# Two-layer encoder: six pairs of each MLP begin with two of their seven products, and the loads, splits and stores around the MLPs are re-timed

## The chip, the cores and the metric

One core of a Trainium2 chip runs the whole program: TensorE (PE, with PEld its weight loads), VectorE (DVE), ScalarE (ACT), GpSimd (POOL), and the queue of SyncE (SP), which issues nearly all DMAs. The metric is the device time of one execution in microseconds (us), lower is better. Durations of single instructions, waits and clocks come from one profiled execution.

## The reference

```python
def reference(x, c, positions, ada_w, ada_b, norm_mix, norm_mlp, mlp_w1, mlp_w2, ...):
    cond = jax.nn.silu(c)
    for i in range(DEPTH):                       # 2 layers, SEQ = 1024, D_MODEL = 1024, D_FF = 4096
        mod = (cond @ ada_w[i] + ada_b[i]).reshape(B, N_MOD, D)
        shift1, scale1, gate1 = ...
        shift2, scale2, gate2 = ...
        h = rms_norm(x, norm_mix[i]) * (1 + scale1) + shift1
        if i % N_MIXERS == 0:
            y = mla_mixer(h, positions, ...)     # layer 0, ends with "@ w_o"
        else:
            y = dilated_mixer(h, positions, ...) # layer 1: three window groups, bias by relative position
        x = x + gate1 * y
        h = rms_norm(x, norm_mlp[i]) * (1 + scale2) + shift2
        x = x + gate2 * (jnp.square(jax.nn.relu(h @ mlp_w1[i])) @ mlp_w2[i])
    return x
```

All tensors are float32.

## The kernel before

**Products.** Each float32 factor is split into a rounded part `hi` (ACT, L114) and a rest `lo` (DVE, L115), and a product is three TensorE passes (lines L383, L384, L385: hi by hi, lo by hi, hi by lo). Such a split is called a form here. A product of 128 columns by 512 tokens over 512 inner elements is 12 matmuls of 128x512.

**The MLP** (`mlp7`) does each 2x2 block product with seven products instead of eight. `prod` names them: L11·R11, L12·R21, S4·R22, L22·T4, S1·T1, S2·T2, S3·T3. In the first phase ("up") the left side is w1 and the right side the normalised input h. A pair is 256 columns of w1 (128 of them in each half); there are 16 pairs, and each takes the seven products in the order L11·R11, S2·T2, L12·R21, S3·T3, S1·T1, L22·T4, S4·R22 (index 0 to 6). S1 to S4 are sums of quarters of w1 (`w_sums`, four DVE operations of 128x512 per pair), T1 to T4 are differences of quarters of h. The sums u of squared results that the second phase needs (`u_sums`, four DVE operations per pair) go to a DRAM scratch `uf` (`u_store`, four DMAs per pair). In the second phase ("down") 56 steps (7 products by 8 groups of w2) each load a part of `uf` ("ufr") and of w2 ("w2r"), split them (`d_form`) and run 24 matmuls.

**The way into the MLP.** `proj_res` is the mixer's last projection. When a tile of 128 tokens is finished it adds the gate and the residual, normalises, and hands out steps made by `h_forms` that transpose and modulate the tile: `first` for the first four tiles, `second` for tiles 4 to 7. `second` computes also all of T1 to T4's differences, and `form`s make the splits of R11, R21, T2, R22, T1, T3, T4. Before, w1 of pairs 0 and 1 is loaded ahead but split behind the projection; pairs 0 and 1 then alternate their products, and from pair 2 on the pairs run one after the other.

**What sets the order.** Code order within each engine's stream, as a scheduler keeps it where an operation is pinned and else by its own choice. Tiles come from a "G" pool of 29 tiles and an "X" pool of 19 (layer 0) or 20 (layer 1), each 128x1024 float32; a new user of a tile waits for the last reader of the old one, and SP issues its DMAs in order, so a store that is not ready holds back the loads behind it.

**Work spread over the MLP of layer 0:** `ada_step` (one 512 KB load "adaw" and one or two DVE operations of 128x1024, the modulation of layer 1), `bias_step` and `write` (DMAs between `bias`, `f` and `bv`, the position bias of layer 1). In the down phase these are a list by step, `fill`. The first three sets of weights of the dilated mixer (`wvr`, `wqkr`) are loaded and split by `dil`, behind the MLP.

Of the kernel before, what the change touches and what calls it, by code (L numbers as in the profile page):

```python
# [41 lines left out]
class K:  # L42
# [284 lines left out]
    def h_forms(self, xs0, xs1, mods, xalloc):  # L327
# [8 lines left out]
        tt = lambda o, x, y: nc.vector.tensor_tensor(o, x, y, op=ALU.subtract)  # L336

        def form(name, src):
            g = [self.G("hf", (P, 2, 512)) for _ in range(2)]
            self.split(*g, src)  # L340
            for k in range(2):
                R.setdefault(name, [[], []])[k].append(g[k])
# [520 lines left out]
    def proj_res(self, O, order, wo, gate, xs, mods, xalloc, done):  # L863
# [4 lines left out]
        with self.tc.tile_pool(name="psO", bufs=6, space=PSUM, reuse_waits="tile") as psp:  # L868
# [29 lines left out]
            for i, (t, b) in enumerate(items):  # L898
# [6 lines left out]
                for _ in range((0, 2, 2, 2, 2, 0, 0, 0)[i]):  # L905
                    steps.pop(0)(psp, "h")
        return at, (at1, steps1)


    def mlp7(self, l, R, steps, xd, out, more=(), nxt=None):  # L910
# [15 lines left out]
        with self.tc.tile_pool(name="psM", bufs=8, space=PSUM, reuse_waits="tile") as psp:  # L926
# [20 lines left out]
            def w_form(L, n):  # L947
                g = self.X("wf", (P, 2, 4, P))
                self.split(g[:, 0], g[:, 1], L[n])
                L[n] = g  # L950

# [3 lines left out]
            def up(u, i):  # L955
# [12 lines left out]
                if i == 0:  # L968
                    u.s1 = self.T("s1")
                    nc.scalar.activation(u.s1, ps, AF.Copy)  # L970
                elif i == 1:
                    u.u2 = self.T("u2")
                    tt(u.u2, ps, u.s1)
                elif i == 2:
                    u.a = self.X("ua", (P, 2, 512), F32)
                    square(u.a[:, 0], ps, u.s1)
# [20 lines left out]
            def u_store(u, c):  # L997
                for n, x in ((("L11", "S1"), u.a), (("L12", "L22"), u.b), (("S3", "S2"), u.s)):
                    nc.sync.dma_start(out=uf[UF[n[0]] : UF[n[0]] + 2, c].rearrange("k p f -> p k f"), in_=x)
                nc.sync.dma_start(out=uf[UF["S4"], c], in_=u.s4)  # L1000
# [45 lines left out]
            def u_forms(c, names):  # L1046
                for n in names:
                    w_form(us[c].L, n)


            us = [Pair() for _ in range(NP)]
            names = [o[0] for o in order]
            raws = {c: w_load(c) for c in range(2)}

            def quarters(c):
                us[c].L = w_quarters(raws.pop(c))
                us[c].q = dict(us[c].L)

            def sums(c):
                w_sums(us[c].L, us[c].q)  # L1060

            for c in range(2):
                quarters(c)
            for n in ("L11", "L12"):
                for c in range(2):
                    u_forms(c, (n,))
            for f in ((0, 0), (1, 0), None, (0, 2), None, (1, 2), None, None):
                if f:
                    up(us[f[0]], f[1])
                else:  # L1070
                    steps.pop(0)(psp, "m")
            for c in range(2):
                sums(c)
                u_forms(c, ("S2",))
            todo = (1, 3, 4, 5, 6)
            for j, i in enumerate(todo):
                up(us[0], i)
                if steps:
                    steps.pop(0)(psp, "m")
                if j < 4:  # L1080
                    for c in range(2):
                        u_forms(c, (names[todo[j + 1]],))
# [709 lines left out]
def program(tc, a):  # L1792
    nc = tc.nc
    with ExitStack() as ctx:
# [35 lines left out]
        with tc.tile_pool(name="bias", bufs=1) as bp:  # L1830
# [17 lines left out]
            for f in fill[16:]:  # L1848
                f.append(write)
# [77 lines left out]
```

## Time and profile before

| | |
|---|---|
| median of 3 runs | 3534.16 us (3531.26 to 3534.18) |
| the profiled execution | 3527.56 us |
| its span on the core | 3525.8 us, mean granted TensorE clock 0.977 |
| TensorE busy | 3330.1 us, 94% |
| VectorE, ScalarE, GpSimd busy | 2476.0, 1769.5, 764.5 us |
| up phase of layer 0, layer 1 | about 835 to 1176 us, 2871 to 3211 us |
| down phase of layer 0, layer 1 | about 1177 to 1518 us, 3211 to 3518 us |
| DMA traffic | 482.91 MB, mean 137 GB/s |

The profile gives, for each instruction group, its line in the source, the busy time and the mean duration of one. "Idle before" is the time its engine stood still just before it, with the engine and line that ended the wait. The table by stages gives for each window the busy time of each engine, the granted clock of TensorE (1.00 is full speed) and the share of the 16 DMA engines in use. "SPq" and "POOLq" are the DMA-issuing queues of SyncE and GpSimd.

### The profile page before, as it was taken

To read this page: it belongs to the slowest core of one execution; us is meant where nothing else is said; L and a number is where in the kernel's file an instruction comes from. 1 tells how busy PE (TensorE), PEld (TensorE's weight loads), DVE (VectorE), ACT (ScalarE), POOL (GpSimd) and SP (SyncE) were. 2 spreads that over 40 slices of the span, in tenths; PEclk is the share of its full clock that TensorE was granted. 3 is DMA by queue.
4 is the path that set the end of the run, shared out by engine and by line. 5 is a ranking of instruction groups with operands and counts; after the bars stand their busy time and mean duration, and the time that the engine had idled before them with its cause. 6 is when DMAs were issued, how large, how long until landed. Compare 5 with 4: busy or idle time off the path is not lost.

```text
span 3525.8 us, 58151 instructions
## 1 busy us (share of the span) xinstructions
PE 3330.1 (94%) x21350; PEld 2971.2 (84%) x21350; DVE 2476.0 (70%) x4860; ACT 1769.5 (50%) x3559; POOL 764.5 (22%) x1299
## 2 busy tenths in 40 slices
PE   6999999897999898989999999999999779999999
PEld 6877788776888786889999999999999668887887
DVE  6678787856887766756667666676778577777666
ACT  5557676744554333535556454564555245454332
POOL 6454444420000000012222222233333200000000
PEclk9999999998999999999999999999999889999999
DMA  5442222241545789533332333332334624447464
GB/s 185 131 163 78 75 93 73 91 138 66 188 170 174 265 211 340 169 88 106 104 99 80 98 106 94 112 87 65 102 97 125 169 84 145 151 162 277 169 213 138
DMA packets 376557, 482.91 MB, mean 137 GB/s; under 512 B 31077, under 2 KB 256658, under 8 KB 376266
## 3 DMA queue, kind: packets, MB, share of 16 engines
q1 hardware_dynamic: 366186, 453.88, 40.3%
q0 software_dynamic: 10080, 25.24, 2.1%
q8 instruction: 171, 2.80, 0.3%
q14 instruction: 120, 0.98, 0.1%
HBM read 348.71 MB, written 118.79 MB: 133 GB/s over the span
## 4 chain that ended last, share of the span: by engine, by line
PE 77%; DVE 6%; DMA 4%; ACT 3%; issue 2%; SPq 0%; POOL 0%; DVEq 0%; ACTq 0%; POOLq 0%
PE psm L385 10%; PE psm L384 10%; PE psm L383 10%; PE psproj L383 8%; PE psproj L385 7%; PE psproj L384 7%; PE pav L804 3%; PE pss L1526 2%; PE ppt L791 2%; PE pspt L1552 2%; PE psq L1495 2%; PE psy L385 2%; PE psy L383 2%; PE psy L384 2%; PE psav L1567 1%
## 5 line engine op out<-in xcount | busy, mean ns | idle before, releaser
L383 PE MATMUL psm<-hf,wf 128*128 128x512 f32 x896 | 354.0, 395 | 24.7 <-ACT wf L114 24.6
L384 PE MATMUL psm<-dl,dh 128*128 128x512 f32 x896 | 354.3, 395 | 11.8 <-DVE dl L115 11.8
L385 PE MATMUL psm<-hf,wf 128*128 128x512 f32 x896 | 351.6, 394 | 11.1 <-DVE wf L115 11.1
L383 PE MATMUL psm<-dh,dh 128*128 128x512 f32 x896 | 339.5, 396 | 18.1 <-ACT dh L114 18.1
L385 PE MATMUL psm<-dh,dl 128*128 128x512 f32 x896 | 352.6, 393 | 0.0
L384 PE MATMUL psm<-hf,wf 128*128 128x512 f32 x896 | 352.5, 393 | 0.0
L383 PE MATMUL psproj<-wqkh,hTp 128*128 128x256 f32 x1024 | 296.8, 290 | 0.0
L385 PE MATMUL psproj<-wqkh,hTp 128*128 128x256 f32 x1024 | 291.5, 285 | 0.0
L384 PE MATMUL psproj<-wqkl,hTp 128*128 128x256 f32 x1024 | 289.9, 283 | 0.0
L114 ACT ACTIVATE dh<-ufr 128x1024 fp32r<-128x1024 f32 x112 | 118.6, 1059 | 284.6 <-DMA ufr<-uf 113.7
L383 PEld LDWEIGHTS psm<-hf,wf 128*128 128x128 f32 x896 | 170.7, 190 | 63.1 <-ACT wf L114 28.3
L383 PEld LDWEIGHTS psm<-dh,dh 128*128 128x128 f32 x896 | 170.1, 191 | 57.8 <-ACT dh L114 21.5
L384 PEld LDWEIGHTS psm<-dl,dh 128*128 128x128 f32 x896 | 170.7, 191 | 50.8 <-DVE dl L115 15.3
L385 PEld LDWEIGHTS psm<-hf,wf 128*128 128x128 f32 x896 | 170.3, 190 | 49.2 <-DVE wf L115 13.7
L115 DVE TENSOR_TENSOR dl<-ufr,dh 128x1024 fp32r<-128x1024 f32 x112 | 136.6, 1220 | 100.5 <-ACT dh L114 86.3
L780 POOL TENSOR_SCALAR p<-p,arl 128x1024 f32<-128x1024 f32 x128 | 145.0, 1133 | 268.9 <-DVE arl L779 204.6
L385 PEld LDWEIGHTS psm<-dh,dl 128*128 128x128 f32 x896 | 170.7, 190 | 35.5
L384 PEld LDWEIGHTS psm<-hf,wf 128*128 128x128 f32 x896 | 170.7, 190 | 35.3
L384 PEld LDWEIGHTS psproj<-wqkl,hTp 128*128 128x128 f32 x1024 | 195.8, 191 | 0.0
L385 PEld LDWEIGHTS psproj<-wqkh,hTp 128*128 128x128 f32 x1024 | 195.6, 191 | 0.0
L1537 ACT ACTIVATE pd<-pd,dnb 128x192 f32<-128x192 f32 (+2 forms) x384 | 168.5, 443 | 54.0 <-DVE dnb L1535 54.0
L383 PEld LDWEIGHTS psproj<-wqkh,hTp 128*128 128x128 f32 x1024 | 195.6, 191 | 0.0
(354 smaller groups left out, 9809.0 us busy)
## 6 DMA issues: line engine op xcount, KB each, us to landing
ufr<-uf SPq DMA_DIRECT2D x112, 512.0 KB, 3.9
adaw<-in_ada_w SPq DMA_DIRECT2D x96, 512.0 KB, 7.1
w2r<-in_mlp_w SPq DMA_DIRECT2D x96, 512.0 KB, 5.0
w1r<-in_mlp_w SPq DMA_DIRECT2D x64, 512.0 KB, 5.8
bt<-bias SPq DMA_DIRECT2D x128, 256.0 KB, 2.7
wqkr<-in_dil_w_in SPq DMA_DIRECT2D x96, 256.0 KB, 4.0
qkv<-st SPq DMA_DIRECT2D x32, 512.0 KB, 3.4
hraw<-qkv SPq DMA_DIRECT2D x32, 512.0 KB, 3.9
```

Of the source, the lines that this page charges most:

```text
L114: nc.scalar.activation(hi, src, AF.Copy)
L115: (lo_eng or nc.vector).tensor_tensor(lo, src, hi.bitcast(F32), op=ALU.subtract)
L383: mm(out, lh, rh, start=first, stop=False)
L384: mm(out, lh, rl, start=False, stop=False)
L385: mm(out, ll, rh, start=False, stop=last)
L780: nc.gpsimd.tensor_scalar(p, p, rl, 1.0, op0=ALU.mult, op1=ALU.mult)
L791: nc.tensor.transpose(pt[:, k * P : (k + 1) * P], u["p"][i][:, kt * P : (kt + 1) * P], self.ident)
L804: nc.tensor.matmul(ps[:, j % 2, :], heads[h]["v"][:, kt, :], u["pT"][hl][kt // 4][:, kt % 4, :], start=kt == 0 and hl == 0, stop=kt == 7 a ...
L1495: nc.tensor.transpose(ps[:, (2 * e + k) * P : (2 * e + k + 1) * P], s4[:, i, e, 64 * k : 64 * k + 128], identr)
L1526: nc.tensor.matmul(ps[:, e * 256 : (e + 1) * 256], q[:, e, k, :], u["k"][:, e, w0 : w0 + 256], start=k == 0, stop=k == 1)
L1537: nc.scalar.activation(p[:, e, lo:hi], p[:, e, lo:hi], AF.Exp, bias=nb[:, e : e + 1], accum_out=stat[g][:, t, 1, 2 * pr + e : 2 * pr + e + 1])
L1552: nc.tensor.transpose(ps[:, (n * e + b) * P : (n * e + b + 1) * P], p[:, e, c : c + P], self.ident)
```

## The change

It is made for both MLPs.

- **Six early pairs.** For pairs 0 to 5 the left half of w1 that the quarters L11 and L12 need is loaded once more by itself ("w1h", 128 columns of all 1024 rows, 512 KB), and split into the G pool. The first three are loaded at step 3 of the projection's second loop and split at its steps 4, 5 and 6 (`more`).
- **Order of products.** `seq`: first L11·R11 and L12·R21 of pairs 0 to 5 (12 products), then the other five products of each of these pairs, then pairs 6 to 15 with seven each. All loads, sums and forms are put by product number: w1 of a pair 12 products ahead, its sums 6 ahead, a form 4 ahead.
- **T2 first.** `second` computes only T1's and T2's difference and the form of T2; the differences of T3 and T4 are in `others`, with the forms of T3, T1, T4, R22. The steps stand at products 2, 3 (`second`), 5, 7, 8, 10 (`others`). These operations are pinned.
- **Stores of u** go out from GpSimd's queue.
- **Down phase.** Loads are issued three steps ahead instead of two, the first four near the end of the up phase, the first two forms at its last two products. The loads of x for the residual are spread over four steps, the gate comes at group 4.
- **Layer 0's extra work.** Up phase: one `ada_step` for pairs 3 to 15. Down phase: `ada_step` at steps 8 to 40, none at 0 to 7; bias steps at 8 and 13 instead of 1 and 6; writes at 16 to 23 and 40 to 47 instead of from 16 on.
- **Dilated weights.** `wv` loaded at down step 51 and split at 53, `wqk` loaded at 54.

```diff
         def second(psp, tag, dp):
-            t1, t4 = keep[dp], keep[2 + dp]
-            t3, r22, t2 = (xalloc("hs", (P, 2, 512), F32) for _ in range(3))
-            rs.append((t3, r22))
+            t1 = keep[dp]
+            t3, r22 = (xalloc("hs", (P, 2, 512), F32) for _ in range(2))
+            t2 = self.G("ht2", (P, 2, 512), F32)
+            rs.append((t3, r22, t2))
...
             tt(t1, t3, t1)
             tt(t2, r22, t1)
-            form("T2", t2)
-            tt(t3, r22, t3)
-            tt(t4, t4, t2)
+            form("T2", t2, True)
 
         def others(name):
-            for src in {"T3": [r[0] for r in rs], "T1": keep[0:2], "T4": keep[2:4], "R22": [r[1] for r in rs]}[name]:
-                form(name, src)
+            for dp in range(2):
+                t3, r22, t2 = rs[dp]
+                if name == "T3":
+                    tt(t3, r22, t3)
+                elif name == "T4":
+                    tt(keep[2 + dp], keep[2 + dp], t2)
+                form(name, {"T3": t3, "T1": keep[dp], "T4": keep[2 + dp], "R22": r22}[name], True)
...
+    def w1_half(self, l, c):
+        src = self.a["mlp_w1"][l].rearrange("(d p) f -> p d f", p=P)[:, :, c * 256 : c * 256 + P]
+        return self.load(src, (P, 8, P), "w1h")
+
+    def w1_form(self, src, alloc):
+        g = alloc("wf", (P, 2, 4, P))
+        self.split(g[:, 0], g[:, 1], src)
+        return g
...
             def u_store(u, c):
                 for n, x in ((("L11", "S1"), u.a), (("L12", "L22"), u.b), (("S3", "S2"), u.s)):
-                    nc.sync.dma_start(out=uf[UF[n[0]] : UF[n[0]] + 2, c].rearrange("k p f -> p k f"), in_=x)
-                nc.sync.dma_start(out=uf[UF["S4"], c], in_=u.s4)
+                    nc.gpsimd.dma_start(out=uf[UF[n[0]] : UF[n[0]] + 2, c].rearrange("k p f -> p k f"), in_=x)
+                nc.gpsimd.dma_start(out=uf[UF["S4"], c], in_=u.s4)
...
+            seq = [(c, i) for c in range(E) for i in (0, 2)]
+            seq += [(c, i) for c in range(NP) for i in range(7) if c >= E or i not in (0, 2)]
...
+            for c in range(E):
+                if eloads[c]:
+                    put(2 * c - 5, eloads[c])
+                if eforms[c]:
+                    put(2 * c - 3, eforms[c])
+            for n, f in zip((2, 3, 5, 7, 8, 10), steps):
+                put(n, f, psp, "m")
+            for c in range(NP):
+                put(first[c] - 12, quarters, c)
+                put(first[c] - 6, quarters, c)
+                for i in range(7):
+                    if not (c < E and i in (0, 2)):
+                        put(at[(c, i)] - 4, form, c, i)
+                put(at[(c, 6)] + 2, u_sums, us[c])
+                put(at[(c, 6)] + 4, u_store, us[c], c)
+                if l == 0 and 2 < c < NP:
+                    put(at[(c, 4)], self.ada_step, psp, "m")
+            for k in range(4):
+                put(N - 6 + k, d_first, k, False)
+            for k in range(2):
+                put(N - 2 + k, d_first, k, True)
...
-                if n + 2 <= last:
-                    ld[n + 2] = d_load(*dsteps[n + 2])
-                for k in {last - 2: (last - 1, last), last - 1: (), last: ()}.get(n, (n + 1,)):
+                if n > 0 and n + 3 <= last:
+                    ld[n + 3] = d_load(*dsteps[n + 3])
+                for k in {0: (), last - 2: (last - 1, last), last - 1: (), last: ()}.get(n, (n + 1,)):
...
-            fill = [[k.ada_step] if n < 8 or n >= 16 else [] for n in range(54)]
+            fill = [[k.ada_step] if 8 <= n < 41 else [] for n in range(56)]
...
-            for n in (1, 6):
+            for n in (8, 13):
                 fill[n].append(bias_step)
-            for f in fill[16:]:
+            for f in fill[16:24] + fill[40:48]:
                 f.append(write)
+            fill[51].append(lambda *x: got.update(wv=k.dil_weights("v", 0, 0)))
+            fill[53].append(lambda *x: got.update(wv=got["wv"]()))
+            fill[54].append(lambda *x: got.update(wqk=k.dil_weights("qk", 0, 0)))
...
-            k.mlp7(1, forms, steps, xm[1], store, [[k.ada_step]] * 8 + [[]] * 8 + [[k.ada_step]] * 3)
+            k.mlp7(1, ea, forms, steps, xm[1], store, [[]] * 8 + [[k.ada_step]] * 11)
```

**Where it moves instructions, first place: ACT at the end of layer 0's projection.** Lines L259, L104, L105 normalise one tile of tokens (xh); L114 wf is the rounded part of a quarter of w1, from `w1r` (256 columns) or `w1h` (128 columns). Before:

```order
L259 ACTIVATE xh_15230,xms_15229<-x_14675 128x1024
L104 ACTIVATE xrl_15233<-xms_15229,eps 128x1
L105 ACTIVATE xry_15232<-xrl_15233 128x1
L259 ACTIVATE xh_15273,xms_15272<-x_14677 128x1024
L104 ACTIVATE xrl_15276<-xms_15272,eps 128x1
L105 ACTIVATE xry_15275<-xrl_15276 128x1
L259 ACTIVATE xh_15316,xms_15315<-x_14679 128x1024
L104 ACTIVATE xrl_15319<-xms_15315,eps 128x1
L105 ACTIVATE xry_15318<-xrl_15319 128x1
L114 ACTIVATE wf_15347<-w1r_15339 128x512
L114 ACTIVATE wf_15350<-w1r_15343 128x512
```

Now:

```order
L340 ACTIVATE hf_15203<-hk_15195 128x1024
L114 ACTIVATE wf_15207<-w1h_15141 128x512
L114 ACTIVATE wf_15210<-w1h_15141 128x512
L114 ACTIVATE wf_15256<-w1h_15143 128x512
L114 ACTIVATE wf_15259<-w1h_15143 128x512
L114 ACTIVATE wf_15305<-w1h_15145 128x512
L114 ACTIVATE wf_15308<-w1h_15145 128x512
L259 ACTIVATE xh_15242,xms_15241<-x_14675 128x1024
L104 ACTIVATE xrl_15245<-xms_15241,eps 128x1
L105 ACTIVATE xry_15244<-xrl_15245 128x1
L259 ACTIVATE xh_15291,xms_15290<-x_14677 128x1024
```

Six splits of w1 that stood behind the normalisation of the last tile stand ahead of that of the last three tiles.

**Second place: DVE in the first products of layer 0's MLP.** L336 are the differences of quarters of h, L115 (now also L341) hf the rests of their forms, L919 (now L955) ws the sums of w1's quarters and ua results of products. Before:

```order
L919 TENSOR_TENSOR ua_15489<-psm_15476,s_3169_15387 128x512
L919 TENSOR_TENSOR ws_15509<-w1r_15339,w1r_15341 128x512
L919 TENSOR_TENSOR ws_15510<-w1r_15339 128x512
L336 TENSOR_TENSOR hk_15189<-hk_15189,hs_15443 128x1024
L115 TENSOR_TENSOR hf_15471<-hs_15443,hf_15470 128x1024
L115 TENSOR_TENSOR hf_15494<-hs_15389,hf_15493 128x1024
L919 TENSOR_TENSOR ws_15509<-ws_15509,w1r_15339 128x512
L115 TENSOR_TENSOR hf_15498<-hs_15441,hf_15497 128x1024
L115 TENSOR_TENSOR hf_15502<-hk_15039,hf_15501 128x1024
L115 TENSOR_TENSOR hf_15506<-hk_15084,hf_15505 128x1024
L919 TENSOR_TENSOR ws_15510<-w1r_15341,ws_15509 128x512
```

Now:

```order
L336 TENSOR_TENSOR hk_15084<-hs_15456,hk_15084 128x1024
L955 TENSOR_TENSOR ws_15558<-w1r_15363,w1r_15365 128x512
L955 TENSOR_TENSOR ws_15559<-w1r_15363 128x512
L336 TENSOR_TENSOR ht_3189_15458<-hs_15457,hk_15084 128x1024
L955 TENSOR_TENSOR ws_15558<-ws_15558,w1r_15363 128x512
L955 TENSOR_TENSOR ua_15518<-psm_15542,ua_15518 128x512
L955 TENSOR_TENSOR ws_15559<-w1r_15365,ws_15558 128x512
L341 TENSOR_TENSOR hf_15486<-ht_3189_15458,hf_15485 128x1024
L115 TENSOR_TENSOR wf_15520<-w1h_15454,wf_15520 128x512
L115 TENSOR_TENSOR wf_15523<-w1h_15454,wf_15523 128x512
L336 TENSOR_TENSOR hs_15400<-hs_15401,hs_15400 128x1024
L955 TENSOR_TENSOR ua_15577<-psm_15593,ua_15577 128x512
```

The sums of the first pair stand before the last form of T2 now, and the long operations on h are taken apart by short ones on w1 and on results.

**Third place: SP's queue at the end of layer 0's up phase.** L999 and L1000 are stores of u, L234 an `ada_step`'s load, L389 (now L396) the loads of u and w2. Before:

```order
L999 DMA uf_15335<-ub_17899 128x2x512
L999 DMA uf_15335<-ua_17867 128x2x512
L999 DMA uf_15335<-us_17949 128x2x512
L1000 DMA uf_15335<-us_3616_17950 128x512
L234 DMA adaw_17959<-in_ada_w 128x1024
L389 DMA ufr_17962<-uf_15335 128x2x512
L389 DMA w2r_18055<-in_mlp_w 128x2x512
L389 DMA w2r_18057<-in_mlp_w 128x2x512
L389 DMA w2r_18097<-in_mlp_w 128x2x512
L389 DMA w2r_18099<-in_mlp_w 128x2x512
```

Now:

```order
L234 DMA adaw_17890<-in_ada_w 128x1024
L396 DMA ufr_17893<-uf_15359 128x2x512
L396 DMA w2r_17895<-in_mlp_w 128x2x512
L396 DMA w2r_17897<-in_mlp_w 128x2x512
L396 DMA w2r_18006<-in_mlp_w 128x2x512
L396 DMA w2r_18008<-in_mlp_w 128x2x512
L396 DMA w2r_18045<-in_mlp_w 128x2x512
L396 DMA w2r_18047<-in_mlp_w 128x2x512
L396 DMA w2r_18084<-in_mlp_w 128x2x512
L396 DMA w2r_18086<-in_mlp_w 128x2x512
```

The stores are gone from this queue (GpSimd issues them), and the loads of w2 no longer stand behind the last pair's results.

More of the change, by code (lines that the diff above doesn't have):

```diff
@@ L861, in wo_load, with proj_res @@
         return self.wsplit(src, (P, 2, 512), "wo", alloc=alloc)
-    def proj_res(self, O, order, wo, gate, xs, mods, xalloc, done):
+    def proj_res(self, O, order, wo, gate, xs, mods, xalloc, done, more):
         nc = self.nc
@@ L906, in proj_res, with mlp_early, load, form @@
                     steps.pop(0)(psp, "h")
+                for f in more.get(i, ()):
+                    f()
         return at, (at1, steps1)
-    def mlp7(self, l, R, steps, xd, out, more=(), nxt=None):
+    def w1_half(self, l, c):
[5 more added lines that the diff above has]
+        return g
+    def mlp_early(self, l, E):
+        Ls, raws = [{} for _ in range(E)], {}
+        def load(c):
+            raws[c] = self.w1_half(l, c)
+        def form(c):
+            raw = raws.pop(c)
+            for g in range(2):
+                Ls[c][f"L1{g + 1}"] = self.w1_form(raw[:, 4 * g : 4 * g + 4, :], self.G)
+        return Ls, [lambda c=c: load(c) for c in range(E)], [lambda c=c: form(c) for c in range(E)]
+    def mlp7(self, l, early, R, steps, xd, out, more=(), nxt=None):
         nc, a = self.nc, self.a
@@ L1044, in down @@
                     self.mm3(ps, uh[:, k, ts], ul[:, k, ts], wh[:, k, :], wl[:, k, :], first and k == 0, last and k == 1)
-            def u_forms(c, names):
-                for n in names:
-                    w_form(us[c].L, n)
+            Ls, eloads, eforms = early
+            E = len(Ls)
             us = [Pair() for _ in range(NP)]
[L1052 to L1074, printed above, removed]
@@ L1167, in mlp7 @@
                     ps = [M() for _ in range(4)]
[L1168 to L1172 removed]
+                if i in (3, 5) and gr < 4:
+                    t = i * 2 - 6 + gr
+                    xs[t] = self.load(xd[t * P : (t + 1) * P, :], (P, 1024), "x")
+                if (i, gr) == (3, 4):
+                    g = self.gate(l, 1)
                 if (i, gr) == (5, 5) and nxt is not None:
@@ L1826, in program, with early @@
         keep_x = lambda l: (lambda t: nc.gpsimd.dma_start(out=xm[l][t * P : (t + 1) * P, :], in_=xs[t]))
-        forms, (_, steps) = k.proj_res(O, (4, 5, 0, 1, 2, 3, 6, 7), wo, gate, xs, mods(0, 3), k.X, done=keep_x(0))
+        got = {}
+        def early(l, E=6, n=3):
+            Ls, loads, forms = k.mlp_early(l, E)
+            hooks = {3: loads[:n]}
+            for c in range(n):
+                hooks[4 + c] = [forms[c]]
+            return (Ls, [None] * n + loads[n:], [None] * n + forms[n:]), hooks
+        ea, hooks = early(0)
+        forms, (_, steps) = k.proj_res(O, (4, 5, 0, 1, 2, 3, 6, 7), wo, gate, xs, mods(0, 3), k.X, keep_x(0), hooks)
         xd = k.dp.tile([S, D], F32, name="xd")
@@ L1856, in program @@
         wo = {0: [], 1: []}
-        got = {}
         def tail():
@@ L1873, in program @@
                 nc.sync.dma_start(out=xs[t][p0 : p0 + n, :], in_=s)
-        forms, (_, steps) = k.proj_res(O, range(8), wo, got["gate"], xs, mods(1, 3), k.X, done=keep_x(1))
+        ea, hooks = early(1)
+        forms, (_, steps) = k.proj_res(O, range(8), wo, got["gate"], xs, mods(1, 3), k.X, keep_x(1), hooks)
         def store(t, c, x, eng):
```

168 lines of the change are left out of this document (75 added, 93 removed).

## The prediction
> **What bounds the kernel now.** I read the page's first part, then the table by stages around the MLPs, then TensorE's waits, its timeline and the chain of waits there, and last the DMA rows.
>
> ```profile
> PE 3330.1 (94%) x21350; PEld 2971.2 (84%) x21350; DVE 2476.0 (70%) x4860; ACT 1769.5 (50%) x3559; POOL 764.5 (22%) x1299
> ```
>
> TensorE is busy 94% of the span. The change leaves its number of matmuls as it is, so only time in which it stands still, or runs slowly after standing still, can be won. That time lies in six stretches:
>
> ```profile
> 830.00:880.00 50.00, 31.97 (x128) 24.43 (x127) 37.90 (x48) 26.77 (x40) 0.53 (x1) 0.76 0.14 45
> 1160.00:1215.00 55.00, 45.23 (x178) 35.81 (x177) 43.16 (x55) 18.86 (x22) 0.00 (x0) 0.88 0.77 279
> 1300.00:1360.00 60.00, 48.38 (x192) 36.84 (x191) 25.07 (x25) 12.82 (x13) 0.00 (x0) 0.91 0.98 289
> 1495.00:1535.00 40.00, 28.30 (x135) 23.76 (x134) 26.84 (x36) 17.89 (x27) 1.48 (x3) 0.87 0.40 130
> 2866.00:2912.00 46.00, 28.27 (x114) 21.15 (x113) 36.79 (x47) 26.76 (x40) 0.53 (x1) 0.78 0.23 76
> 3195.00:3230.00 35.00, 27.00 (x102) 21.06 (x102) 26.37 (x27) 14.90 (x17) 0.00 (x0) 0.85 0.94 355
> ```
>
> Length less PE busy is TensorE's idle time: **A** (layer 0, projection to MLP) 18.0 us, **C** (up to down) 9.8, **D** (middle of down) 11.6, **E** (MLP to dilated mixer) 11.7, **B** (layer 1, projection to MLP) 17.7, **F** (up to down) 8.0. Together 76.8 us. The column after POOL is the granted clock: 0.76 to 0.91 here. The timeline and the chain of waits of A show what that costs and why it waits:
>
> ```profile
> 862.42 0.80 PE L383 MATMUL psm<-hf,wf 128*128 128x512 f32 x1 [8.39 <-ACT wf L114]
> 863.01 0.63 PE L384 MATMUL psm<-hf,wf 128*128 128x512 f32 x1
> 868.71 0.80 PE L385 MATMUL psm<-hf,wf 128*128 128x512 f32 x1 [5.07 <-DVE wf L115]
> ```
> ```profile
> 841.97 0.43 PE psm L384
> 842.40 2.06 PE pst L290 x16
> 844.46 0.24 PE psm L383
> 844.71 0.23 PE psm L384
> ...
> 852.20 1.24 DVE hk L336
> ...
> 858.83 2.27 DVE hf L115 x2
> 861.10 0.60 DVE ws L919
> 861.70 3.41 DVE hf L115 x3
> 865.11 1.80 DVE ws L919 x3
> 866.91 1.14 DVE hf L115
> 868.05 0.61 DVE wf L115
> ```
>
> A matmul takes 0.43 us after a wait and 0.23 us otherwise, so a slow one costs 0.20. In A the timeline has 13 slow ones from 836.91 and 11 from 868.71: 24 x 0.20 = 4.9 us. Busy time x (1 - clock) would be 31.97 x 0.24 = 7.7 there, so I take 4.9/7.7 = 0.64 of that figure elsewhere: C 3.5, D 2.8, E 2.4, B 4.0, F 2.6. Slow matmuls cost about 20 us, and **97 us are at stake**.
>
> **The change part by part.** Durations come from the one profiled execution (3527.56 us, span 3525.8). The median of the runs is 3534.16, 6.6 us more; the sum is made against 3527.6.
>
> *A and B.* The wait of 8.39 us is for a quarter sum's split, and 5.07 for its rest. VectorE was never idle: long operations on h (1.14 us each: 3.41 for three) stood in its queue ahead of short ones on w1 (0.60: 1.80 for three). The first products need R11 and R21 alone. Before, four such products (10.9 us with 12 x 0.227 each) covered the making of T2; now twelve do, 12 x 12 x 0.227 = 32.7 us, plus 32 transposes at 2.06 for 16 = 4.1, so from about 832 to 869. VectorE reached T1's difference at 852.2; from there T1 and T2 (four operations) and the two rests of T2's form are 6 x 1.14 = 6.8 us, with some ten short ones 13 us: 865, ahead of 869, and sooner where the first half is transposed sooner. The first wait, 3.8 + 0.7 us for splits that stood behind the last normalisation, goes because three pairs are split within the projection.
>
> What is late next: T3, T1, T4, R22 want 12 x 1.14 = 13.7 us of VectorE while five products last 13.6. Over the whole stretch to pair 5's end TensorE has 42 x 2.72 + 4 = 118 us of work; VectorE has 18 x 1.14 = 20.5, some 128 short operations x 0.60 to 0.64 = 77 to 82, and in layer 0 three `ada_step`s of 1.2: 98 to 106 us, or 83 to 90%. It fits, but not in every product. From nothing to 10 us per layer; I take 3 where T forms follow each other and 2 in the pairs behind. A: 18.0 + 4.9 - 5 = **18**; B: 17.7 + 4.0 - 5 = **17**. The extra loads (12 x 0.5 MB) come where DMA share is 0.14 to 0.23 in A and B's rows, and cost nothing unless they hold a tile; the six splits ahead of the last three normalisations in ACT (0.6 each, 3.6 us) are covered by the same twelve products, and cost up to 3.6 without them.
>
> *C and F.*
>
> ```profile
> SPq L999 <- ACT ub L966: 11.8, 1, 11.8
> ```
> ```profile
> 1174.13 2.58 SPq L389 DMA_DIRECT2D w2r<-in_mlp_w  x4
> ```
> ```profile
> 1180.00:1190.00 10.00, 8.47 (x37) 6.63 (x35) 7.06 (x7) 3.62 (x4) 0.00 (x0) 0.96 1.05 393
> ```
>
> SP's queue stood 11.8 us at a store of u, and so issued four loads of w2 only at 1174.13, when the up phase ended at about 1176; from there the DMAs were full (1.05, 393 GB/s). A down step of the first eight loads 0.5 MB of u, 1 MB of w2 and 0.5 MB of adaw in 5.45 us (24 x 0.227): 367 GB/s, nearly all that row shows. Now the stores are in another queue, the loads can start some 10 to 20 us earlier, as soon as TensorE frees X tiles, and without adaw in steps 0 to 7 the need is 275 GB/s. I leave 2 us in each: C 9.8 + 3.5 - 2 = **11**, F 8.0 + 2.6 - 2 = **9** (ends: 4 and 13).
>
> The store itself has no row on GpSimd. The nearest, issues with KB and us to landing:
>
> ```profile
> xm<-x POOLq DMA_DIRECT2D x16, 512.0 KB, 3.2
> oT<-oTd POOLq DMA_DIRECT2D x12, 512.0 KB, 13.0
> oT<-moTd POOLq DMA_DIRECT2D x8, 512.0 KB, 8.8
> xd<-x POOLq DMA_DIRECT2D x12, 256.0 KB, 3.2
> ```
> ```profile
> uf<-ua SPq DMA_DIRECT2D x32, 512.0 KB, 4.2
> ```
> ```profile
> 1470.00:1500.00 30.00, 30.00 (x150) 25.03 (x148) 30.00 (x41) 18.34 (x26) 2.16 (x4) 1.00 0.62 211
> ```
>
> From 3.2 (the same size and direction) to 13.0 us; SP's own store took 4.2. I take 3.2 to 4.2, and no cost: xd's stores fall in 1470 to 1500, where VectorE is busy 30.00 of 30 us, and still land in 3.2. The Trainium skill ("SBUF — State Buffer", section "SBUF: two separate sides") speaks against this edit: GpSimd writes the descriptors of its own DMAs, and is locked out while VectorE runs an operation in a two-port mode, which a float32 copy within SBUF sets off. By that rule the stores would be late whenever VectorE is so occupied; the rows of xd show no lateness, and the groups of the chain above are TENSOR_TENSOR rather than copies. I give the rule a small chance, below.
>
> *D.*
>
> ```profile
> 1329.90 11.90 DMA f<-bv
> ...
> 1341.86 12.40 DMA w2r<-in_mlp_w
> ```
> ```profile
> 1340.00:1350.00 10.00, 4.76 (x15) 3.83 (x16) 3.94 (x4) 2.11 (x2) 0.00 (x0) 0.66 1.07 330
> ```
>
> ```profile
> w2r<-in_mlp_w SPq DMA_DIRECT2D x96, 512.0 KB, 5.0
> ```
>
> The chain there is DMA after DMA: a bias write, then a w2 load of 12.4 us, against a median of 5.0 for w2r, with the DMA share above 1. Before, one write stood in each of steps 16 to 31, beside x, gate and adaw. Now eight of the 16 go to steps 40 to 47; x is spread, and loads are issued a step (5.45 us) earlier. But eight writes still stand ahead of step 24, and adaw's loads stay. Between 0 and all of it stays; I leave 5: 11.6 + 2.8 - 5 = **9**. Steps 40 to 47 have room (DMA share 0.62 in the row of 1470 to 1500).
>
> *E.*
>
> ```profile
> 1521.18 6.94 DMA wvr<-in_dil_w_in
> 1528.15 1.06 ACT wvh L114
> ```
>
> TensorE waited 11.2 us for these weights, issued at 1521.18 behind the MLP's last rows. Loaded at step 51 they are there some 15 us before. Next late is the transposes of tiles 4 to 7, whose normalisation ends at about 1527; 96 matmuls on the first tiles, which start 0.12 us apart in the timeline, 11.5 us, cover that from 1518. The price: two rests of the split (2 x 1.2 us) enter VectorE while it is busy 30.00 of 30, and delay down's last steps by about as much. I leave 4: 11.7 + 2.4 - 4 = **10** (ends 5 and 14).
>
> *Sum:* 18 + 17 + 11 + 9 + 9 + 10 = **74 us**: 3527.6 - 74 = 3453.6 for a profiled execution. Set against the median it would be 3460; between the two I say **3456 us**.
>
> **The rivals.**
>
> 1. *VectorE becomes the bound behind the projection.* The T forms come one product apart, and the 13.7 us of T3 to R22 show on TensorE as gaps between the products of pair 0, with slow matmuls behind each. For: 37.90 us busy of 50 in A, most of the idle rest at its start. Against: the sum of 83 to 90%. Price: 13.7 more per layer and 5 for the clock, less the 5 left already: 2 x 14 = 28, so 3484.
> 2. *The stores from GpSimd are late, and the kernel is slower.* Four stores end a pair's life in the X pool, in 7 x 2.72 = 19.0 us. If GpSimd handles them one after the other, they keep up as long as one takes under 19.0/4 = 4.75 us. At the 8.8 of oT's row a pair would last 35 us, and 26 pairs would lose 16 each, over 400 us; the loss exceeds the gain of 74 from 5.5 us per store on (4 x 5.5 - 19 = 3, x 26 = 78). Just above that, at 6 us, it is 5 x 26 = 130 less 74: 3590. Against: 3.2 in both rows of stores; oT's are loads, in another stage. This is also the way in which the Trainium skill's rule of the shared port would come out.
> 3. *The DMA stalls only move.* D stays whole (the eight writes ahead of step 24 make a stall of the same size, or those at 40 to 47 do) and C and F keep half: 9 + 10 = 19 lost, 3475.
> 4. *The change doesn't do what it says*: the early halves of w1 wait for G tiles, arrive late, and ACT, which keeps its order, holds the last normalisations behind them. A and B then stay: 35 lost, 3491. Against: before A DMA share is low (0.14 within it), and the tiles are freed by TensorE's first loop in the projection, some 20 us ahead of need.
>
> **How the numbers follow.** The forecast's own range, 3430 to 3472 (nothing left in the pairs and E's and C's upper ends, or 4 us more left in four places), gets 0.60. Rival 1 has 0.14, rival 3 has 0.10, rival 4 has 0.09, rival 2 has 0.04, and 0.03 is for nothing gained on balance. The range 3428 to 3496 reaches from nearly all of the 97 us to rival 4. About 0.2%, or 7 us, is what a measurement of this kernel can tell from no change; faster gets the forecast and rivals 1, 3 and 4, 0.93; same 0.03; slower 0.04.
>
> **What would show it.** A and B right: in the table by stages TensorE is busy at least 45 of 50 us behind each projection, and no wait over 2 us for a w1 split; wrong (rival 1): waits on VectorE's hf or wf rests of 1 to 3 us each between products 13 and 25. C and F right: w2r issued 10 us or more before up ends, no wait over 2 us at the first down steps. The stores: uf rows under POOLq with under 4.75 us to landing; wrong if w1r issues wait for them. D: the wait near step 28 at most 5 us, none at 40 to 47. E: psproj follows the last psm within 1 us. The prediction is wrong as a whole if TensorE's busy time grows (its clock falls elsewhere), or if waits of the same sum stand in other places.

## The result, and the profile after

| | before | changed |
|---|---|---|
| median | 3534.17 us (3531.26 to 3534.22, 4 runs) | 3446.89 us (3443.34 to 3447.82, 4 runs) |
| profiled execution | 3527.56 us | 3447.27 us |
| its span | 3525.8 us | 3444.2 us |

The ratio is 0.9753 with a 95% interval of 0.9736 to 0.9770: 87 us less by the medians, 80.3 by the profiled executions. The forecast was 3456 us, from a sum of 74 us to be won.

The first part of the changed kernel's page, busy time and share of each engine:

```profile
PE 3307.4 (96%) x21350; PEld 2957.7 (86%) x21350; DVE 2472.4 (72%) x4860; ACT 1767.1 (51%) x3559; POOL 856.0 (25%) x1427
```

TensorE's instructions are the same 21350, and it is busy 22.7 us less (3330.1 before): so much less time goes to slow matmuls behind waits. It also stands idle 59 us less: 3444.2 - 3307.4 = 136.8 against 3525.8 - 3330.1 = 195.7. Together that is the 81.6 us by which the span fell.

The table by stages of the changed kernel, around A, C, D, E, B and F in the order of the prediction's table (length, busy time of PE, PEld, DVE, ACT, POOL, granted clock, DMA share, GB/s):

```profile
825.00:885.00 60.00, 57.65 (x264) 47.68 (x264) 48.62 (x72) 39.09 (x66) 1.13 (x3) 0.97 0.39 127
1130.00:1185.00 55.00, 52.53 (x229) 42.56 (x228) 45.45 (x53) 22.96 (x27) 4.66 (x7) 1.00 0.97 353
1265.00:1325.00 60.00, 55.18 (x227) 43.57 (x226) 35.16 (x34) 18.64 (x18) 0.00 (x0) 0.94 1.01 322
1425.00:1485.00 60.00, 56.15 (x275) 45.20 (x274) 51.36 (x67) 30.93 (x42) 3.11 (x6) 1.00 0.48 159
2810.00:2860.00 50.00, 48.18 (x222) 39.64 (x221) 37.78 (x57) 31.58 (x53) 1.60 (x3) 0.97 0.33 106
3115.00:3150.00 35.00, 33.15 (x147) 27.13 (x146) 26.62 (x30) 12.89 (x17) 4.01 (x6) 1.00 1.04 391
```

| | idle before | left by the forecast | idle left |
|---|---|---|---|
| A, layer 0 projection to MLP | 18.0 | 3, and 2 in the pairs | 2.4 |
| B, layer 1 projection to MLP | 17.7 | 3, and 2 in the pairs | 1.8 |
| C, layer 0 up to down | 9.8 | 2 | 2.5 |
| D, middle of down | 11.6 | 5 | 4.8 |
| E, MLP to dilated mixer | 11.7 | 4 | 3.9 |
| F, layer 1 up to down | 8.0 | 2 | 1.9 |
| sum | 76.8 | 23 | 17.2 |

The longest waits that are left, in TensorE's timeline (start, duration, then in brackets the idle time before and what ended it), and the DMA ahead of the longest in the chain of waits:

```profile
864.00 0.80 PE L390 MATMUL psm<-hf,wf 128*128 128x512 f32 x1 [2.35 <-ACT wf L114]
...
1147.80 0.50 PE L391 MATMUL psm<-dl,dh 128*128 128x512 f32 x1 [1.77 <-DVE dl L115]
...
1315.66 2.07 PE L390 MATMUL psm<-dh,dh 128*128 128x512 f32 x4 [4.82 <-ACT dh L114]
```
```profile
1297.40 17.07 DMA w2r<-in_mlp_w
```

At 864.00 the last early pair's products wait for the split of its half of w1, which stands in ACT's queue behind a form of T3. The wait that ends at 1315.66 is for a load of w2, 17.07 us in the chain, at the same place as before (12.40 then). In the other pairs of the up phases, from 885 to 1130 and from 2860 to 3115 us, TensorE never waits.

### The profile page after: what moved, and what is told of

Same layout as the page of the kernel before. It is cut to its first block, busy times and chain, and to the rows that moved or that the text cites. A ratio compares the mean times of both kernels' runs of the same rounds, so it can differ in the third digit from the quotient of the medians.

```text
span 3444.2 us, 58101 instructions
## 1 busy us (share of the span) xinstructions
PE 3307.4 (96%) x21350; PEld 2957.7 (86%) x21350; DVE 2472.4 (72%) x4860; ACT 1767.1 (51%) x3559; POOL 856.0 (25%) x1427
## 4 chain that ended last, share of the span: by engine, by line
PE 56%; DVE 2%; ACT 1%; DMA 1%; issue 1%; SPq 0%; POOL 0%; DVEq 0%; ACTq 0%; POOLq 0%
PE psproj L390 8%; PE psproj L392 8%; PE psproj L391 8%; PE psm L390 7%; PE psm L391 7%; PE psm L392 7%; PE pss L1558 2%; PE pspt L1584 2%; PE psq L1527 2%; PE psav L1599 1%; PE psav L1600 1%; PE psy L390 1%; PE psk L1535 1%; PE psy L391 1%; PE psy L392 1%; DMA w2r<-in_mlp_w 1%
## 5 line engine op out<-in xcount | busy, mean ns | idle before, releaser
L114 ACT ACTIVATE dh<-ufr 128x1024 fp32r<-128x1024 f32 x112 | 118.4, 1057 | 195.9 <-PE psm L391 45.9
L1512 POOL TENSOR_TENSOR qn<-qn,dgain 128x128 f32<-128x128 f32 x192 | 89.8, 489 | 405.1 <-DVE qn L1509 374.8
```

The lines of the kernel that those rows point to most:

```text
L114: nc.scalar.activation(hi, src, AF.Copy)
L1512: nc.gpsimd.tensor_tensor(qq[:, i], qq[:, i], gain[:, g : g + 1, :].broadcast_to([P, 2, 64]), op=ALU.mult)
```

## The experiments

Twelve kernels ran, each timed in five rounds beside the kernel before. A variant is set against the changed kernel by its ratio to before: the changed kernel itself has 0.9750 in such a run (x0), and 0.001 is 3.5 us.

| run | what it is | ratio to before, 95% interval | median, us |
|---|---|---|---|
| x0_changed | the changed kernel | 0.9750 (0.9736 to 0.9763) | 3440.20 |
| x4_split_late | early splits behind the projection | 0.9788 (0.9775 to 0.9801) | 3453.17 |
| x3_three_pairs | three early pairs | 0.9813 (0.9799 to 0.9826) | 3463.35 |
| x2_sums_early | T3's and T4's differences early | 0.9778 (0.9765 to 0.9792) | 3450.23 |
| x1_store_sync | u stored from SP | 0.9743 (0.9730 to 0.9756) | 3438.96 |
| x5_ada_first8 | adaw in down steps 0 to 7 | 0.9816 (0.9802 to 0.9829) | 3463.16 |
| x6_sync_ada | both of these | 0.9819 (0.9805 to 0.9832) | 3467.46 |
| p1_before_ada | before, no adaw in steps 0 to 7 | 0.9930 (0.9917 to 0.9944) | 3505.85 |
| x7_writes16 | all bias writes at 16 to 31 | 0.9761 (0.9747 to 0.9774) | 3446.04 |
| x9_ahead_two | down loads two steps ahead | 0.9802 (0.9789 to 0.9816) | 3459.64 |
| x8_dil_late | dilated weights behind the MLP | 0.9778 (0.9764 to 0.9791) | 3451.48 |
| b_all | stores on SP, T3 later, adaw and writes moved | 0.9706 (0.9693 to 0.9720) | 3427.55 |

### The changed kernel again

> The changed kernel itself, beside the other kernels of this call, so that they can be set against it on one chip: a ratio to the kernel before of about 0.975. Its wait of 4.8 us in the middle of layer 0's down phase was 1.6 to 2.0 us in four relatives of it; if that wait is a matter of how DMAs fall in one execution it is now anywhere from 1 to 5 us, if it belongs to the kernel it is 4.8 us again.

TensorE's waits in the middle of layer 0's down phase (in total, times, longest):

```profile
PE psm L390 <- ACT dh L114: 1.1, 1, 1.1
```

It was 4.8 us in the first profile. The same kernel has 1.1 to 4.8 us there, so a difference of that size at this place says nothing.

### A and B: early splits, six pairs, T2 first

```diff
-            for c in range(n):
-                hooks[4 + c] = [forms[c]]
-            return (Ls, [None] * n + loads[n:], [None] * n + forms[n:]), hooks
+            return (Ls, [None] * n + loads[n:], forms), hooks
...
+        if alloc == self.G:
+            self.pinned(self.nc.scalar.activation(g[:, 0], src, AF.Copy))
+            self.pinned(self.nc.vector.tensor_tensor(g[:, 1], src, g[:, 0].bitcast(F32), op=ALU.subtract))
```

> The changed kernel with the first three pairs' halves of w1 loaded as early, but split behind the last normalisation (both parts of these splits kept in the order of the code). Prediction's step: the first waits of 3.8 and 0.7 us and the 13 slow matmuls behind them come back in both layers, (4.5 + 2.6) x 2 = 14 us more. Rival, that the order of products took these waits away: within 3 us.

Its timeline at the first product of layer 0's MLP:

```profile
835.03 0.80 PE L390 MATMUL psm<-hf,wf 128*128 128x512 f32 x1 [3.82 <-DVE xry L109]
835.62 0.63 PE L391 MATMUL psm<-hf,wf 128*128 128x512 f32 x1
```

The wait of before is back to the hundredth (3.82 us, and again in layer 1), with slow matmuls behind it. Its row names xry, the last normalisation, where the row of before named a split. In ACT's queue the first split starts at 834.36, right behind that normalisation, and the first product follows at 835.03. 0.9788 against 0.9750 is 13 us; 14 were expected.

```diff
-        def early(l, E=6, n=3):
+        def early(l, E=3, n=3):
```

> The changed kernel with three early pairs instead of six: six products of R11 and R21 ahead of T2 instead of twelve. Theory that the cover has to be twelve products: six of them and the transposes end at about 852, T2's form is ready at 855 and T3, T1, T4, R22 follow each 2 to 5 us later, so TensorE waits 8 to 15 us behind each projection, with slow matmuls behind the waits: 15 to 35 us more. Rival, that the order of the long operations (T2 first, the others spread) does it alone: at most 4 us more.

Its waits behind layer 0's projection (835 to 905 us):

```profile
PE psm L391 <- DVE hf L341: 4.9, 4, 3.5
PE psm L390 <- ACT hf L340: 3.4, 5, 1.7
PE psm L392 <- DVE wf L115: 0.8, 1, 0.8
```

Nine us of waits in many pieces (as much again behind layer 1's projection), now for the forms of h (hf) themselves, and 0.0063 or 22 us in the time. The order alone does not do it; the early products do. The edit takes two things away together, though. The steps that make T3, T1, T4 and R22 stay at products 5, 7, 8 and 10, where these forms are now used at products 7 to 10 instead of 13 to 16, so R22's form is made in the very product that needs it. Three pairs with these steps moved forward were not run.

```diff
             form("T2", t2, True)
+            tt(t3, r22, t3)
+            tt(keep[2 + dp], keep[2 + dp], t2)
...
-                if name == "T3":
-                    tt(t3, r22, t3)
-                elif name == "T4":
-                    tt(keep[2 + dp], keep[2 + dp], t2)
```

> The changed kernel with the differences of T3 and T4 made in the same two steps as T1 and T2 again (four more operations of 1.14 us on VectorE ahead of or beside T2's form). Theory that the twelve products give the cover: T2's last rest was ready at 854.87 in the changed kernel and its first use comes about 14 us later, so 4.6 us more change nothing, within 2 us of 3447. Rival, that T2 first is what removed the waits of 8.4 and 5.1 us: 8 to 25 us more over both layers.

Waits in the same stretch:

```profile
PE psm L388 <- ACT wf L114: 4.3, 2, 2.7
```

4.3 us instead of 2.4 in layer 0, and as much in layer 1. They are not for T2: the early pairs' splits are late. The time is 0.0028 or 10 us up, near the lower end of the rival's 8 to 25: not nothing, as the theory had it, and far from the 27 us that the two waits for S2's split had been in the two layers. The waits account for 4 to 5 of these 10 us. With the slow matmuls behind them the two places are 7 us longer than in x0's trace, of 8.4 us between the two profiled executions; some 2 us are in the middle of layer 0's down phase, where executions of one kernel differ. T2 first helps a little once the twelve products are there, as the early pairs' splits are less late with it.

### C and F: the stores, and adaw

```diff
-                    nc.gpsimd.dma_start(out=uf[UF[n[0]] : UF[n[0]] + 2, c].rearrange("k p f -> p k f"), in_=x)
-                nc.gpsimd.dma_start(out=uf[UF["S4"], c], in_=u.s4)
+                    nc.sync.dma_start(out=uf[UF[n[0]] : UF[n[0]] + 2, c].rearrange("k p f -> p k f"), in_=x)
+                nc.sync.dma_start(out=uf[UF["S4"], c], in_=u.s4)
```

> The changed kernel with one part undone: u is stored from SP's queue again. If the stores on SP held up the loads of w2 (the prediction's reading of C and F, 9.8 and 8.0 us of waits before), about half of what C and F won comes back: 8 to 16 us more than the changed kernel's 3447, with new waits over 2 us at the first down steps. Rival: the earlier place of the first loads and the missing adaw in steps 0 to 7 did it, and then it stays within 3 us. A third theory, that stores from GpSimd cost something, expects it faster by over 3 us.

Its table by stages around C and F:

```profile
1130.00:1185.00 55.00, 54.27 (x238) 44.31 (x237) 46.43 (x55) 24.13 (x29) 0.00 (x0) 1.00 1.01 370
3110.00:3150.00 40.00, 40.00 (x178) 33.10 (x178) 34.37 (x37) 19.25 (x23) 0.00 (x0) 1.00 1.02 379
```

With the stores back on SP TensorE stands still for 0.7 and 0.0 us, less than with GpSimd's (2.5 and 1.9). The time is the same within the interval (0.9743 against 0.9750). The theory that stores on SP held up the loads falls. The third theory isn't excluded: it would be 3 to 4 us by these two stretches, and the interval can't tell that from nothing.

```diff
-            fill = [[k.ada_step] if 8 <= n < 41 else [] for n in range(56)]
+            fill = [[k.ada_step] if n < 33 else [] for n in range(56)]
...
-        k.mlp7(1, ea, forms, steps, xm[1], store, [[]] * 8 + [[k.ada_step]] * 11)
+        k.mlp7(1, ea, forms, steps, xm[1], store, [[k.ada_step]] * 8 + [[]] * 8 + [[k.ada_step]] * 3)
```

> The changed kernel with one ada_step in each of down steps 0 to 7 again (and none at the end of the stretch, in both layers). Prediction's reading: with adaw a step needs 367 of the 393 GB/s that the DMAs gave, so the waits at the first down steps grow, 3 to 8 us in each layer, 6 to 16 us in all. Rival: the loads were issued early enough, and the time stays within 3 us of the changed kernel.

Its table by stages behind C and F, and the chain of waits in F (start, duration, what):

```profile
1150.00:1185.00 35.00, 31.30 (x129) 25.38 (x128) 28.67 (x28) 13.21 (x14) 2.27 (x4) 0.90 0.99 373
3135.00:3165.00 30.00, 18.06 (x72) 14.51 (x73) 24.07 (x25) 10.31 (x12) 2.72 (x4) 0.83 0.98 374
```
```profile
3126.44 11.11 DMA w2r<-in_mlp_w
...
3137.61 14.95 DMA w2r<-in_mlp_w
```

The DMAs are full (0.98 to 0.99, 374 GB/s), loads of w2 take 11 and 15 us in the chain, and TensorE stands still 3.7 us behind C and 11.9 behind F. 0.9816 against 0.9750 is 23 us, above the expected 6 to 16; a wait of 6.4 us in the middle has its part in that (some 5 us, at the place where executions of one kernel differ), and 18 us are left for the two places.

A load that takes 11 us isn't the difference by itself. These are the loads of w2 in F, from 3110 to 3165 us, with the median from issue to landing, first in the changed kernel and then in x5:

```profile
w2r<-in_mlp_w SPq DMA_DIRECT2D x19, 512.0 KB, 10.9
```
```profile
w2r<-in_mlp_w SPq DMA_DIRECT2D x15, 512.0 KB, 11.0
```

The changed kernel's loads are as slow, and its longest wait there is 1.8 us. The edit also moves more than a load: an `ada_step` has an operation on VectorE and holds a tile of the X pool. Which of the three costs most was not taken apart. The chain points to the DMAs: from 3120 to 3165 us loads of w2 are 57.9% of it, VectorE's sum of adaw 2.0%.

> Both ways out of the first down steps undone: u stored from SP again, and an ada_step in each of steps 0 to 7 again. If adaw's traffic alone made the waits, the place of the stores does nothing here either: a ratio to before of 0.980 to 0.983, as with adaw alone (0.9816). If stores on SP and adaw hold up the loads together, as the prediction had it, 5 to 15 us more than that: 0.983 to 0.986.

This kernel has both diffs. 0.9819 against 0.9816: the place of the stores does nothing here either.

```diff
-            fill = [[k.ada_step] if n < 8 or n >= 16 else [] for n in range(54)]
+            fill = [[k.ada_step] if 8 <= n < 50 else [] for n in range(54)]
...
-            k.mlp7(1, forms, steps, xm[1], store, [[k.ada_step]] * 8 + [[]] * 8 + [[k.ada_step]] * 3)
+            k.mlp7(1, forms, steps, xm[1], store, [[]] * 8 + [[k.ada_step]] * 11)
```

> The kernel before with one part of the change alone: no ada_step in down steps 0 to 7, those go to the steps behind (8 on in layer 0 and 8 to 18 in layer 1). If adaw's traffic was the cause of C and F, 8 to 20 us less than before (ratio 0.994 to 0.998) with the waits at the first down steps mostly gone. Rival, the stores on SP and the late loads: within 3 us of before.

The kernel before with this alone, around C and F:

```profile
1150.00:1205.00 55.00, 54.91 (x247) 44.58 (x245) 44.53 (x62) 24.35 (x28) 0.00 (x0) 1.00 0.90 312
3180.00:3215.00 35.00, 32.19 (x135) 25.87 (x134) 28.57 (x30) 18.59 (x22) 0.00 (x0) 0.95 0.95 354
```

C's 9.8 us of waits are 0.1, F's 8.0 are 2.8, and the kernel is 25 us faster by the runs (0.9930), above the expected 8 to 20, and 20 by the profiled spans (3525.8 and 3506.1). The stores still go out from SP here, and the loads are issued as late as before (four at 1174.13 then, eight from 1173.67 on here). This edit alone is a quarter or more of what the whole change won.

### D: writes, and distance of the loads

```diff
-            for f in fill[16:24] + fill[40:48]:
+            for f in fill[16:32]:
```

> The changed kernel with all 16 bias writes at down steps 16 to 31 again. Prediction's reading: the eight writes in steps 24 to 31 made the DMA jam in the middle, so a wait of 5 to 10 us comes back near step 28, with slow matmuls, 5 to 10 us more. Rival: the spread of x's loads and the earlier loads did it, within 3 us.

```profile
PE psm L390 <- ACT dh L114: 5.1, 1, 5.1
PE psm L391 <- DVE dl L115: 0.9, 1, 0.9
```

6.0 us of waits in the middle (1270 to 1335 us). The changed kernel alone has 1.1 to 4.8, x8 below, which changes nothing at this place, 5.7, and the intervals of the times overlap (0.9761 and 0.9750): the writes' place is worth a few us at most, and the run can't tell it from nothing.

```diff
-            for k in range(4):
+            for k in range(3):
                 put(N - 6 + k, d_first, k, False)
...
-                if n > 0 and n + 3 <= last:
-                    ld[n + 3] = d_load(*dsteps[n + 3])
+                if n > 0 and n + 2 <= last:
+                    ld[n + 2] = d_load(*dsteps[n + 2])
```

> The changed kernel with the loads of a down step issued two steps ahead again instead of three. In the kernel before the middle of layer 0's down phase lost 11.6 us in waits, in the changed one 1.1 to 4.8, and all 16 writes at 16 to 31 gave 6.0. If the step more of distance made the difference, waits of 8 to 12 us come back there, 4 to 10 us more than the changed kernel (ratio 0.976 to 0.978). Rival: the spread of x's loads and the writes did it, and the ratio stays at 0.974 to 0.976 with waits of 1 to 5 us.

TensorE's waits in the middle (1280 to 1345 us), and the chain of waits there:

```profile
PE psm L390 <- ACT dh L114: 10.0, 1, 10.0
PE psm L391 <- DVE dl L115: 4.6, 3, 2.0
```
```profile
1292.69 10.30 DMA bias<-bv
1303.02 9.80 DMA x<-xm
1312.88 15.69 DMA w2r<-in_mlp_w
```

The chain of the kernel before is back, DMA behind DMA, with 14.6 us of waits, and 0.0052 or 18 us in the time; some 3 us of that are a wait of 3.25 us behind C, which came back too. The step more of distance made the difference in D. The writes and x's loads are spread in this kernel, and that did not help without it.

### E: the dilated weights

```diff
-            fill[51].append(lambda *x: got.update(wv=k.dil_weights("v", 0, 0)))
-            fill[53].append(lambda *x: got.update(wv=got["wv"]()))
-            fill[54].append(lambda *x: got.update(wqk=k.dil_weights("qk", 0, 0)))
...
-        wts[("v", 0, 0)] = wv
-        loads[2] = wqk
-        fetch_split(2)
+        for f in (0, 1, 2):
+            fetch(f)
+            fetch_split(f)
```

> The changed kernel with the first dilated weights loaded and split behind the MLP again. Prediction's term: 10 us more (the wait of 11 us for wvh comes back, the two rests of the split leave the last down steps). Rival: with the end of down lighter in other ways, the loads land in time and only 0 to 3 us come back.

```profile
1490.17 0.79 PE L390 MATMUL psproj<-wvh,hT 128*128 128x256 f32 x2 [10.23 <-ACT wvh L114]
```

The wait is back, and 0.0028 or 10 us, as expected. TensorE's waits on VectorE's rests in the last 60 us of down tell something else. In order: before (1458 to 1518), the changed kernel (1418 to 1478), x8 (1420 to 1480) and x9 (1434 to 1494):

```profile
PE psm L384 <- DVE dl L115: 0.5, 1, 0.5
```
```profile
PE psm L391 <- DVE dl L115: 1.7, 4, 1.1
```
```profile
PE psm L391 <- DVE dl L115: 1.6, 4, 1.0
```
```profile
PE psm L391 <- DVE dl L115: 1.2, 1, 1.2
```

The change brought these waits, and they stay when the dilated weights leave (x8). With the loads two steps ahead (x9) three of the four are gone.

### What was left

```diff
-            for n, f in zip((2, 3, 5, 7, 8, 10), steps):
+            for n, f in zip((2, 3, 7, 8, 9, 10), steps):
...
-            fill = [[k.ada_step] if 8 <= n < 41 else [] for n in range(56)]
+            fill = [[k.ada_step] if 8 <= n < 24 or 31 <= n < 48 else [] for n in range(56)]
...
-            for f in fill[16:24] + fill[40:48]:
+            for f in fill[14:22] + fill[40:48]:
```

With these edits u is stored from SP, by x1's diff.

> The changed kernel, u stored from SP, the form of T3 made two products later (at product 7), so that ACT splits pair 5's half of w1 ahead of it, no ada_step in down steps 24 to 30, and the first eight bias writes at 14 to 21. Expected from the waits left: 2.4 + 1.8 us and some 2 us of slow matmuls behind the projections, about 4 us at the first down steps, 1 to 5 us in the middle: 8 to 14 us less than the changed kernel, a ratio of 0.971 to 0.973. Rival: VectorE, at 88% there, shows the same waits at other products, and the DMA jam moves: within 3 us of the changed kernel, 0.974 to 0.976.

Its page and its table by stages around A, C, D, B and F:

```profile
PE 3299.0 (96%) x21350; PEld 2953.2 (86%) x21350; DVE 2470.3 (72%) x4860; ACT 1766.4 (52%) x3559; POOL 765.3 (22%) x1299
```
```profile
828.00:888.00 60.00, 60.00 (x280) 49.20 (x279) 47.15 (x71) 40.33 (x67) 1.60 (x3) 1.00 0.41 131
1130.00:1185.00 55.00, 54.23 (x239) 44.25 (x238) 46.46 (x55) 23.63 (x29) 0.00 (x0) 1.00 1.01 369
1255.00:1325.00 70.00, 70.00 (x306) 56.47 (x305) 39.98 (x38) 25.30 (x25) 0.00 (x0) 1.00 0.87 291
2803.00:2863.00 60.00, 59.18 (x278) 48.94 (x277) 49.95 (x69) 41.12 (x65) 0.53 (x1) 1.00 0.31 103
3100.00:3140.00 40.00, 40.00 (x178) 33.11 (x178) 35.18 (x37) 19.75 (x24) 0.00 (x0) 1.00 1.02 385
```

Of the 13.3 us that were left in these five places 1.6 remain (0 + 0.8 + 0 + 0.8 + 0), and the granted clock is 1.00 in all five. The 4.8 us in D are in part a matter of the execution (x0 had 1.1), and what each of the four edits did was not taken apart. At 0.9706 it is the fastest kernel here, 15 us under the changed one, a little more than expected, and 103 under before.

## Why the prediction was right, and which steps failed

**Idle time as the stake: right, but too small.** 97 us were put at stake, of them 20 for slow matmuls behind waits. The matmuls cost 22.7 us less in the changed kernel, and 31.1 less in b_all (3330.1 and 3299.0 us busy, the same 21350 matmuls). So 20 was low by some 11 us. The step that failed is the factor of 0.64: without it the same six rows give 31.4 us. What was left over by place was forecast as 23 us and measured 17.2.

**Place by place.** Take for every matmul the time to the start of the next one, less what a matmul of its kind usually takes; that counts idle time and slow matmuls together. By this count, before against changed, the change won 20.8 us in A, 20.5 in B, 14.4 in C, 8.4 in D, 7.6 in E and 10.1 in F. These six make 81.8 us, and the span fell by 81.6, so next to nothing was won or lost elsewhere. The forecast had 18, 17, 11, 9, 10 and 9: A, B and C were low by about 3 each, E was high by 2.

**A and B: right, by their own step.** Cover, with the lead that it gives the forms (x3), and early splits (x4) are each shown by taking them away, and x4's price of 14 us was met with 13. The sum of VectorE's work gave 83 to 90% of the stretch, and no wait on VectorE came in the pairs: the 2 us per layer that were set aside there were not needed. T2's form was ready earlier than the step had it: its last operation starts at 853.65 against a forecast of 865, because the halves are transposed between the early products. Rival 1 did not occur; with three early pairs (x3) waits of its kind came, 10 to 11 us a layer by the count above against its price of 14. One sign was missed: no wait over 2 us for a split of w1 was to be left, and one of 2.35 us is.

**C and F: the amount near, half of the cause wrong.** The step "SP's queue stood 11.8 us at a store of u, and so issued four loads of w2 only at 1174.13" reads a true row for a cause. Its place is misread too: down's first matmul starts at 1166.54, not at about 1176, and loads of w2 had gone out before that.

```profile
1148.83 2.24 SPq L389 DMA_DIRECT2D w2r<-in_mlp_w  x4
```

x1 and p1 show that the queue's wait was harmless: stores on SP cost nothing in the changed kernel, and in the kernel before the waits of C go with adaw alone, the stores where they were. The other half of the step, adaw's share of the demand, was the cause: p1 alone wins 16.9 us in C and 7.4 in F by the count above, of 14.4 and 10.1 that the whole change won. It was not priced apart from the stores; alone it is worth 18 us in x5 and 20 to 25 in p1, as much as the 20 that the two places were to win together. The amount held because one change undid both halves, which is luck. The sum of the demand was low as well: it took 512 KB for 0.5 MB, while the profile counts 10^6 bytes to the MB. Four loads of 524288 bytes in 5.45 us are 385 GB/s, 98% of the 393, not 367 (three are 289, not 275). So with adaw the stage had next to nothing to spare, and waits of 3.7 and 11.9 us came in x5, with a granted clock of 0.90 and 0.83.

**D: the amount right, the weight wrong.** The step put "eight of the 16 go to steps 40 to 47" first and the step more of distance last. x7 and x9 turn that round: the writes' place isn't told from nothing, the distance is worth some 15 us there. It isn't free, see E. That a jam was left was right, and its size differs between executions of one kernel.

**E: the wait right, the price put on the wrong part.** 10 us were forecast and 10 came back in x8, but the change as a whole won 7.6 there. What is left (3.9 us) is mostly small waits in down's last steps, in the timeline from 1433 to 1457, and 0.8 before the first psproj. The step took such waits for the price of the two dilated splits, and x8, which has no such splits there, shows nearly the same. With the loads two steps ahead (x9) the stretch is 3.6 us shorter by the count, so the cost belongs to the third step of distance, which the forecast gave no price. How the distance makes VectorE's rests late there is not shown.

**The stores from GpSimd.** They landed in 3.4 to 4.6 us, below the 4.75 us from which rival 2 would have decided. Neither the rival nor any gain came: x1's time is equal within the interval.

**Against the median.** The sum of 74 us was set against both the profiled execution and the median, and taken between them. By the medians 87 us were won, by the profiled executions 80, by their spans 81.6. Against the spans the sum is 7.6 us low: A and B kept 4.2 us of idle time instead of the 10 left to them, and slow matmuls gave 22.7 instead of 20.

## What to carry to other kernels

A wait in a queue of DMAs that stands just ahead of a stall isn't yet its cause: add up what the stage moves per step, and where that comes near to what the DMAs gave at their fullest, take traffic out of the stage before moving issues between queues. Count it in the profile's own unit. When a stage starts on fresh operands whose making needs a chain of another engine's work, put independent work in front that is as long as the chain, and count that engine's whole queue, not the chain alone. Count the slow matmuls behind the waits too: here they were a quarter of the gain. And loads issued further ahead can help one stretch and cost another: here the middle of down won some 15 us and its end lost about 4.

## What the runs showed of the hardware that was not expected

A full DMA share does not by itself make TensorE wait. Sixty us in the middle of layer 0's down phase, by stages, in the changed kernel's second execution (x0) and with the loads two steps ahead (x9):

```profile
1265.00:1325.00 60.00, 58.81 (x253) 46.56 (x252) 36.79 (x35) 20.16 (x20) 0.00 (x0) 1.00 1.02 336
```
```profile
1280.00:1340.00 60.00, 45.45 (x181) 35.01 (x180) 30.96 (x30) 15.82 (x16) 0.00 (x0) 0.91 0.91 290
```

The DMAs moved more per second where TensorE stood still 1.2 us (336 GB/s, share 1.02) than where it stood still 14.6 (290 GB/s, 0.91): here one step of distance decided whether a full queue was felt.

The issue rows of the stores of u, from GpSimd in x0 and from SP in x1 (KB, median us to landing):

```profile
uf<-ub POOLq DMA_DIRECT2D x32, 512.0 KB, 4.6
uf<-ua POOLq DMA_DIRECT2D x32, 512.0 KB, 3.6
uf<-us POOLq DMA_DIRECT2D x32, 512.0 KB, 4.7
uf<-us POOLq DMA_DIRECT2D x32, 256.0 KB, 4.4
```
```profile
uf<-ub SPq DMA_DIRECT2D x32, 512.0 KB, 3.1
uf<-ua SPq DMA_DIRECT2D x32, 512.0 KB, 2.9
uf<-us SPq DMA_DIRECT2D x32, 512.0 KB, 7.0
uf<-us SPq DMA_DIRECT2D x32, 256.0 KB, 2.8
```

Three of the four land 0.7 to 1.6 us later from GpSimd, the fourth 2.3 us sooner; the rule of the Trainium skill weighed in the prediction ("SBUF — State Buffer", section "SBUF: two separate sides") isn't contradicted, since VectorE's work beside these stores is nearly all TENSOR_TENSOR with no copy among it, and no run tried it beside copies. GpSimd is also busy 92 us more with issuing them (856.0 against 764.5 us before), which showed in no time measured here.
